# Modulation in quarters, projections behind each quarter, a summed square for two token blocks

## The chip, the cores and the metric

The kernel runs on one core of one Trainium2 chip. The metric is device time in microseconds (us) of one launch, the median of the runs. Before the change it is 1892.64 us (three runs, 1891.05 to 1894.15).

## The reference

One layer of a diffusion backbone runs over 256 context tokens and 2048 latent tokens of 1024 channels. The modulation gives one shift, scale and gate per channel, one set for the latent tokens (from `c`) and one for the context (from `c_ctx`). The input is normalised, scaled and shifted, and projected by one wide matrix; a state-space branch and a convolution branch follow, and an output projection.

```python
silu_ctx, silu_c = silu(c_ctx)[None, :], silu(c)
mod_ctx = silu_ctx @ w_mod[l] + b_mod[l]          # (1, 3*1024); mod_lat the same with silu_c

def trunk_layer(x, mod, grid, h0, ...):
    shift, scale, gate = split(mod, 3)
    h = rms_norm(x, g_pre) * (1 + scale) + shift  # x * rsqrt(mean(x*x) + EPS) * g_pre ...
    u = h @ w_in
    z, xbc, dt_raw, ga, gb, gsil = split(u, ...)
    y_ssd, h_fin = ssd_branch(z, xbc, dt_raw, ...)
    y_conf = conformer_branch(ga, gb, ...) * silu(gsil)
    out = concatenate([y_ssd, y_conf]) @ w_out
    return x + gate * rms_norm(out, g_post), h_fin
```

## The kernel before

Tokens are held in blocks, channels on the 128 partitions. Block 0 is the 256 context tokens; blocks 1 to 4 are 512 latent tokens each. The first half of the program works on blocks 1, 2 and 0, in that order. The 1024 input channels are eight tiles of 128, counted by `k`.

`hprep` (L241) makes the input `h` of one block. Its eight tiles `ht` are loaded (L253), multiplied by the reciprocal root mean square of their tokens (VectorE, L288; the factors stand in a PSUM bank `pr`, which TensorE fills at L278 from the `rstd` columns `xr` that GpSimd makes at L128), scaled and shifted by the modulation `S1` and `SH` (ScalarE, L289), and split into a rounded part `hh` (VectorE, L281) and the rest `hl` (L282, GpSimd, every fourth on VectorE). For block 1 the mean squares come from the tiles themselves: ScalarE squares each (L260), and TensorE sums its partitions with four matmuls against ones (L262, 64 trace records for the block). For all other blocks they come from the same tokens in the other layout: `xin` (L205, 512 KB for each 128 tokens), squared and summed along the row by ScalarE in one instruction (L272).

`modulation(h)` (L207) makes half of the scales and shifts, 512 channels of each. It loads eight 512 KB pieces `wm` of `w_mod`, multiplies them on TensorE into `mp` (L222), copies `mp` out (L228), turns it with eight small transposes into `mc` (L231) and adds the biases on VectorE (L235 to L237).

A projection unit, `xbc_unit` (L434), takes one weight tile and runs 24 matmuls per block (`mm_cm`, L361 to L363: for each `k` the products hh·wh, hl·wh and hh·wl) into a bank `xp`; ScalarE copies that out to `raw` (L446). The weight arrives as two halves `wr` (L335) and is split into `wh` (ScalarE, L336) and `wl` (GpSimd, L337), which are also written to DRAM for later (`whd`, `wld`, L338 and L339). `dt_block` (L299) runs 16 more matmuls per block into `pd` (L306, L307), whose transposes are `pdt` (L316).

At the start (L857 to L888) the order in which the steps are called is written out by hand: the squares of block 1, the first half of the modulation, four tiles of `h`, the second half, and two projection units (`first[0]`, `first[1]`) stepped between. The third unit and `pd` for block 1 come in `xbc_phase` (L466), where the three units go through blocks 2 and 0 while those blocks are prepared. A scheduler turns the calls into one fixed list per engine; each engine works its list strictly in order and waits on semaphores. All loads and stores are issued by SyncE (SP), also in one fixed order, and an issue waits until the eighth transfer before it has landed. `dcol` (L881) is a pair of 2 KB loads made of single 4-byte elements.

Of the kernel before, what the change touches and what calls it, by code (L numbers as in the profile page):

```python
# [67 lines left out]
def backbone_kernel(ctx, tc, xa, xt_in, cols, rows, wconv, conf_b, gp_row, bg_row, state0, w_mod, w_dt, w_in, w_out,  # L68
# [138 lines left out]
    def modulation(h):  # L207

        mp = bank("mm", f"mp{h}")
        for k in range(KT):  # L210
            if h == 1 and k in (4, 5):
                wm = pa.tile([P, 2, 512], F32, tag=("xT", "el")[k - 4], name=f"wm{h}_{k}", bufs=1)
            elif h == 1 and k > 5:
                wm = cp.tile([P, 2, 512], F32, tag="x4", name=f"wm{h}_{k}", bufs=3)
            else:
                w = 2 if h else 4
                if k % w == 0:
                    wms = hps[0 if h else 2].tile([P, w, 2, 512], F32, tag="ab"[k // w], name=f"wm{h}_{k}")
                wm = wms[:, k % w]
            DMA.dma_start(wm, w_mod[k * P:(k + 1) * P, 0:2 * D].rearrange("p (s c) -> p s c", s=2)[:, :, h * 512:(h + 1) * 512])  # L220
            for s in range(4):
                T.matmul(mp[32 * s:32 * s + 2, 0:256], sc[:, :, k], wm[:, s // 2, s % 2 * 256:s % 2 * 256 + 256],  # L222
                         start=(k == 0), stop=(k == KT - 1))
            yield
        mc = bank("ss", f"mc{h}")
        mr = slab(f"mr{h}")
        for s in range(4):
            (V.tensor_copy if s % 2 else S.copy)(mr[0:2, s * 256:(s + 1) * 256], mp[32 * s:32 * s + 2, 0:256])  # L228
            for q in range(2):
                c = 2 * s + q  # L230
                T.transpose(mc[:, 2 * c:2 * c + 2], mr[0:2, c * P:(c + 1) * P], ident[0:2, 0:2])  # L231
        m = mc[:, 0:16].rearrange("p (s k a) -> p s a k", s=2, k=4)
        ks = slice(4 * h, 4 * h + 4)
        bc4 = lambda c: cv[:, c + 4 * h:c + 4 * h + 4].unsqueeze(1).to_broadcast([P, 2, 4])
        V.scalar_tensor_tensor(S1[:, :, ks], m[:, 1], 1.0, bc4(C_BSC), ADD, ADD)  # L235
        V.tensor_tensor(S1[:, :, ks], S1[:, :, ks], bc4(C_GPRE), MUL)
        V.tensor_tensor(SH[:, :, ks], m[:, 0], bc4(C_BSH), ADD)  # L237
        yield


    def hprep(b, out):  # L241
# [13 lines left out]
        if b == 1:  # L255
            pms = [bank("ss", f"pms{t}") for t in range(nt)]
            for k in range(KT):
                load_t(k)
# [1 line left out]
                S.activation(sq, ts[k], AF.Square)  # L260
                for t in range(nt):
                    T.matmul(pms[t][:, 0:1], sq[:, t * P:(t + 1) * P], ones[:, 0:1], start=(k == 0), stop=(k == KT - 1))  # L262
# [2 lines left out]
        for t in range(nt):
            i = o // P + t
            ms = evp.tile([P, 1], F32, tag="ms", name=f"ms{i}", bufs=4)
            if b == 1:
                V.tensor_scalar(ms, pms[t][:, 0:1], 1.0 / D, EPS, MUL, ADD)
            else:  # L270
                xt = xin.pop(i)
                S.activation(xt, xt, AF.Square, accum_out=ms)  # L272
# [6 lines left out]
        def split(k):  # L279
            t = ts.pop(k)  # L280
            V.tensor_copy(hh[:, k, :], t)  # L281
            (V if k % 4 == 3 else G).tensor_tensor(hl[:, k, :], t, hh[:, k, :].bitcast(F32), SUB)  # L282

        for k in range(KT):
            if b != 1:
                load_t(k)
            t = ts[k]
            V.tensor_tensor(t, t, pr[:, :BN], MUL)  # L288
            S.activation(t, t, AF.Identity, bias=SH[:, a, k:k + 1], scale=S1[:, a, k:k + 1])  # L289
            if k > 0 and not (b == 1 and k == 4):  # L290
                split(k - 1)
            if b == 1 and k == 3:
                split(k)
# [571 lines left out]
    for _ in range(4):
        next(prep)
        next(mod)
    next(mod)
    for _ in range(4):
        next(first[0])  # L870
        next(first[1])
        next(mod)
    next(prep)
# [334 lines left out]
```

## Time and profile before

| what | value |
|---|---|
| median of three runs | 1892.64 us (1891.05 to 1894.15) |
| the profiled execution's own time | 1895.74 us |
| its span, first to last instruction | 1894.0 us |
| granted TensorE clock, mean over the span | 0.987 |
| DVE (VectorE), ACT (ScalarE), POOL (GpSimd) busy | 62%, 42%, 33% of the span |
| moved by DMA | 375.30 MB, mean 198 GB/s |

An engine's busy time is the union of its instructions. A timeline row gives start, length, engine, line, tile written and tiles read, and in brackets how long the engine had stood idle and what released it. A time of the span is counted from its first instruction. A matmul's row shows its latency, so the rate is read from one start to the next. The rows that the prediction argues from stand in it.

### The profile page before, as it was taken

The numbers are of one execution on the slowest core, as the hardware profiler recorded it, in microseconds if no ns is written. First come the engines' busy times: TensorE is split into PE (matmuls) and PEld (weight loads), VectorE is DVE, ScalarE is ACT, GpSimd is POOL, SyncE is SP. The second block draws the span as 40 slices with busy tenths as digits, with TensorE's granted clock in tenths as the row PEclk, the third lists the DMA queues.
The fourth block names the chain that finished last, engine by engine and source line by source line (L and its number), as shares of the span: only waits on it lengthen the run. The fifth ranks groups of instructions, "written<-read, shape, count | busy, mean of one in ns | idle before, by whom it ended". The sixth has DMA issues, their size and how long they took to land.

```text
span 1894.0 us, 27057 instructions
## 1 busy us (share of the span) xinstructions
PE 1836.3 (97%) x9739; PEld 1502.5 (79%) x9739; DVE 1174.3 (62%) x1605; ACT 786.4 (42%) x1746; POOL 629.8 (33%) x613
## 2 busy tenths in 40 slices
PE   7999999999999999999999989989999999999998
PEld 5888878888888878888877767767787888888886
DVE  3686873333343443687688778788438677776752
ACT  2546414545444453355245655554314323222321
POOL 2524314445444442301133433342025233333220
PEclk9999999999999999999999999999999999999999
DMA  8656566656566674645777786887777655555532
GB/s 309 224 193 217 200 222 193 200 170 211 191 220 198 219 241 154 190 168 189 195 191 178 235 214 195 248 237 190 240 266 226 200 179 177 159 167 171 171 101 77
DMA packets 290386, 375.30 MB, mean 198 GB/s; under 512 B 85190, under 2 KB 187462, under 8 KB 290252
## 3 DMA queue, kind: packets, MB, share of 16 engines
q1 hardware_dynamic: 290252, 373.58, 63.7%
q8 instruction: 77, 1.26, 0.3%
q14 instruction: 57, 0.47, 0.1%
HBM read 243.92 MB, written 129.59 MB: 197 GB/s over the span
## 4 chain that ended last, share of the span: by engine, by line
PE 66%; DVE 8%; issue 5%; DMA 4%; ACT 2%; POOL 2%; SPq 0%; POOLq 0%; DVEq 0%; ACTq 0%
PE op L1058 19%; PE sp L361 6%; PE sp L362 6%; PE sp L363 6%; DVE cg L573 3%; PE gb L361 2%; PE ga L361 2%; PE ga L362 2%; PE ga L363 2%; PE gb L362 2%; PE gb L363 2%; PE xp L361 2%; PE xp L362 2%; PE xp L363 2%; DMA lb<-lt 2%
## 5 line engine op out<-in xcount | busy, mean ns | idle before, releaser
L361 PE MATMUL sp<-hh,wh 128*128 128x512 f32 (+1 forms) x640 | 239.8, 375 | 0.0
L362 PE MATMUL sp<-hl,wh 128*128 128x512 f32 (+1 forms) x640 | 236.8, 370 | 0.0
L363 PE MATMUL sp<-hh,wl 128*128 128x512 f32 (+1 forms) x640 | 236.5, 370 | 0.0
L668 ACT ACTIVATE lb<-lb,WB 128x128 f32<-128x128 f32 x576 | 181.4, 391 | 97.4 <-POOL lb L660 96.4
L361 PE MATMUL xp<-hh,wh 128*128 128x512 f32 (+1 forms) x480 | 179.1, 375 | 3.8 <-ACT raw L446 2.6
L363 PE MATMUL xp<-hh,wl 128*128 128x512 f32 (+1 forms) x480 | 179.2, 373 | 1.0 <-POOL wl L337 0.6
L362 PE MATMUL xp<-hl,wh 128*128 128x512 f32 (+1 forms) x480 | 179.4, 374 | 0.0
L660 POOL TENSOR_SCALAR_AFFINE_SELECT lb<-lb 128x512 f32<-128x512 f32 x144 | 109.3, 766 | 201.4 <-DMA lb<-lt 127.6
L458 DVE SCALAR_TENSOR_TENSOR cva<-raw,cwh,cva 128x1280 f32<-128x1280 f32 (+1 forms) x96 | 149.2, 1562 | 41.0 <-ACT cva L452 39.3
L337 POOL TENSOR_TENSOR wl<-wr,wh 128x512 fp32r<-128x512 f32 x88 | 129.5, 1484 | 129.6 <-ACT wh L336 119.6
L573 DVE SCALAR_TENSOR_TENSOR cg<-cg,cv 128x256 f32<-128x256 f32 x240 | 138.5, 590 | 3.6
L361 PEld LDWEIGHTS sp<-hh,wh 128*128 128x128 f32 x640 | 121.0, 189 | 22.9 <-issue 3.1
L363 PEld LDWEIGHTS sp<-hh,wl 128*128 128x128 f32 x640 | 120.9, 189 | 20.8
L362 PEld LDWEIGHTS sp<-hl,wh 128*128 128x128 f32 x640 | 121.2, 189 | 19.7
L361 PE MATMUL ga<-hh,wh 128*128 128x512 f32 (+1 forms) x320 | 122.3, 382 | 5.8 <-DMA wh<-whd 5.8
L361 PE MATMUL gb<-hh,wh 128*128 128x512 f32 (+1 forms) x320 | 122.1, 381 | 4.3 <-DVE gth L522 4.3
L533 DVE SCALAR_TENSOR_TENSOR sth<-sth,sp 128x512 f32<-128x512 f32 (+1 forms) x80 | 50.2, 630 | 114.7 <-ACT sth L532 114.6
L362 PE MATMUL ga<-hl,wh 128*128 128x512 f32 (+1 forms) x320 | 120.1, 375 | 0.0
L363 PE MATMUL ga<-hh,wl 128*128 128x512 f32 (+1 forms) x320 | 119.9, 375 | 0.0
L362 PE MATMUL gb<-hl,wh 128*128 128x512 f32 (+1 forms) x320 | 119.8, 374 | 0.0
L363 PE MATMUL gb<-hh,wl 128*128 128x512 f32 (+1 forms) x320 | 119.7, 374 | 0.0
L361 PEld LDWEIGHTS xp<-hh,wh 128*128 128x128 f32 x480 | 91.4, 191 | 20.3 <-ACT raw L446 3.1
(223 smaller groups left out, 4036.7 us busy)
## 6 DMA issues: line engine op xcount, KB each, us to landing
lb<-lt SPq DMA_DIRECT2D x144, 256.0 KB, 4.5
wr<-in_w_in SPq DMA_DIRECT2D x88, 256.0 KB, 4.8
whd<-wh SPq DMA_DIRECT2D x44, 512.0 KB, 3.6
wld<-wl SPq DMA_DIRECT2D x44, 512.0 KB, 4.0
wh<-whd SPq DMA_DIRECT2D x44, 512.0 KB, 5.7
wl<-wld SPq DMA_DIRECT2D x44, 512.0 KB, 5.5
xT<-xb SPq DMA_DIRECT2D x18, 512.0 KB, 5.6
yp<-yg SPq DMA_DIRECT2D x36, 256.0 KB, 4.6
```

The costliest lines, as they stand in the source:

```text
L337: G.tensor_tensor(wl[:, ks, :], wr, wh[:, ks, :].bitcast(F32), SUB)
L361: T.matmul(ps[:, :BN], wh[:, k, :], hh[:, k, :], start=(k == 0), stop=False)
L362: T.matmul(ps[:, :BN], wh[:, k, :], hl[:, k, :], start=False, stop=False)
L363: T.matmul(ps[:, :BN], wl[:, k, :], hh[:, k, :], start=False, stop=(k == KT - 1))
L458: V.scalar_tensor_tensor(a[:, :n], raw[:, t:t + n], cwh[:, ct * 5 + t:ct * 5 + t + 1], a[:, :n], MUL, ADD)
L533: V.scalar_tensor_tensor(th, th, 1.0, ps[:, :BN], ADD, MUL)
L573: V.scalar_tensor_tensor(acc, g[:, t:t + 256], cv[:, w0 + t:w0 + t + 1], acc, MUL, ADD)
L660: G.affine_select(E[g, hq, d], E[g, hq, d], pattern=[[0, 4], [sg, P]], compare_op=ALU.is_ge, fill=NEG, base=0, channel_multiplier=-sg)
L668: S.activation(lb[:, h, :], lb[:, h, :], AF.Exp, bias=WB[:, i, c + h:c + h + 1])
L1058: T.matmul(pso[n], lhs[:, k % 8, :], w[:, n * 512:(n + 1) * 512], start=(k == 0 and m == 0), stop=(k == 15 and m == 2))
```

## The change

The modulation is made in four quarters of 256 channels (two `k` tiles of scale and of shift each). `w_mod` is laid out on the host so that each 512 KB piece is one contiguous 4 KB row per partition, and the gate's third of it becomes an input of its own. The activations `sc` are padded with zeros from 2 to 32 columns, so that each quarter needs one copy `mr` and one 128x128 transpose `mc` where a half had four copies and eight small transposes. For blocks 1 and 2 ScalarE squares the eight tiles, VectorE adds the squares up (seven additions), and four matmuls with ones sum the partitions at the end; block 2 no longer loads its four `xin`. Block 1's multiplication by `pr` is done for all eight tiles ahead of the modulation. Behind each quarter the hand-written order steps the projection units, the third too; no unit is left for `xbc_phase` to step through block 1. `wdr`, `rw` and `dcol` are loaded behind all that.

```diff
-    sc = pa.tile([P, 2, 8], F32, name="sc")
+    sc = pa.tile([P, 32, 8], F32, name="sc")
+    G.memset(sc, 0.0)
...
+    def mod_tiles(q, j):
+        n = f"wm{q}_{j}"
+        if q == 3 and j == 0:
+            return pa.tile([P, 2, 2, 256], F32, tag="xT", name=n, bufs=1)
+        if q == 3 and j == 1:
+            return pa.tile([P, 2, 2, 256], F32, tag="el", name=n, bufs=1)
+        if q == 3:
+            return cp.tile([P, 2, 2, 256], F32, tag="x4", name=n, bufs=3)
...
-    def modulation(h):
+    def modulation(q):
+        mp = bank("ss", f"mp{q}")
+        for j in range(4):
+            wm = mod_tiles(q, j)
+            DMA.dma_start(wm, w_mod[(4 * q + j) * P:(4 * q + j + 1) * P].rearrange("p (k s c) -> p k s c", k=2, s=2))
+            for kk in range(2):
+                k = 2 * j + kk
+                for s in range(4):
+                    T.matmul(mp[32 * s:32 * s + 32, 0:P], sc[:, :, k], wm[:, kk, s // 2, s % 2 * P:s % 2 * P + P],
+                             start=(k == 0), stop=(k == KT - 1))
+        mr = pa.tile([P, P], F32, tag="mr", name=f"mr{q}", bufs=1)
+        V.tensor_copy(mr, mp[:, 0:P])
+        mc = bank("ss", f"mc{q}")
+        T.transpose(mc[:, 0:P], mr, ident)
...
-        if b == 1:
-            pms = [bank("ss", f"pms{t}") for t in range(nt)]
+        if b in (1, 2):
+            sq = ev(f"sq{b}")[:, :BN]
             for k in range(KT):
                 load_t(k)
-                sq = ev(f"sq{k}")[:, :BN]
-                S.activation(sq, ts[k], AF.Square)
-                for t in range(nt):
-                    T.matmul(pms[t][:, 0:1], sq[:, t * P:(t + 1) * P], ones[:, 0:1], start=(k == 0), stop=(k == KT - 1))
+                if k == 0:
+                    S.activation(sq, ts[k], AF.Square)
+                else:
+                    s1 = ev(f"sq{b}_{k}")[:, :BN]
+                    S.activation(s1, ts[k], AF.Square)
+                    V.tensor_tensor(sq, sq, s1, ADD)
+            pms = bank("ss", f"pms{b}")
+            for t in range(nt):
+                T.matmul(pms[:, t:t + 1], sq[:, t * P:(t + 1) * P], ones[:, 0:1], start=True, stop=True)
...
+        if b == 1:
+            for k in range(KT):
+                scale(k)
+            yield
         for k in range(KT):
...
-                    if half == 0 and b == 0 and u is not first[-1]:
+                    if half == 0 and b == 0:
                         continue
...
     next(prep)
-    run(modulation(0))
+    more_w()
+    next(prep)
+    modulation(0)
+    more_w()
+    steps([prep], 2)
+    modulation(1)
+    more_w()
+    steps(first[:2], 2)
+    steps([prep], 2)
+    modulation(2)
+    steps(first[:2], 2)
+    steps(first[2:], 4)
+    steps([prep], 2)
+    modulation(3)
+    steps(first, 2)
+    steps([prep], 2)
+    steps(first, 2)
+    run(prep)
     DMA.dma_start(wdr.rearrange("p k n -> p (k n)"), w_dt)
```

Behind the join named below, the lists of all engines are the same but for a few neighbours that change places. Three pieces of the lists in front of it follow; line numbers in rows of the changed kernel are its own, and a name's first number is the block (in `xin`, `xr` and `ms` the tile of 128 tokens), the second the channel tile; in `xp` and `raw` they are half, unit and block.

ScalarE before, from the first square of block 2's rows (`xin6` is tokens of block 2) to the copies of block 1's first two units:

```order
L272 ACTIVATE xin6_644,ms6_652<-xin6_644 128x1024
L228 COPY mr1_560<-mp1_418 2x256
L336 CAST wh1152_0_474<-wr1152_0_475 128x512
L336 CAST wh1152_0_474<-wr1152_1_479 128x512
L272 ACTIVATE xin7_646,ms7_657<-xin7_646 128x1024
L289 ACTIVATE ht1_4_302<-ht1_4_302,SH_222,S1_221 128x512
L289 ACTIVATE ht1_5_310<-ht1_5_310,SH_222,S1_221 128x512
L289 ACTIVATE ht1_6_318<-ht1_6_318,SH_222,S1_221 128x512
L289 ACTIVATE ht1_7_326<-ht1_7_326,SH_222,S1_221 128x512
```

ScalarE in the changed kernel, the same place, and from there to the last square of block 2:

```order
L287 ACTIVATE xin0_822,ms0_826<-xin0_822 128x1024
L271 ACTIVATE sq2_696<-ht2_0_697 128x512
L274 ACTIVATE sq2_1_702<-ht2_1_700 128x512
L308 ACTIVATE ht1_6_296<-ht1_6_296,SH_222,S1_221 128x512
L308 ACTIVATE ht1_7_301<-ht1_7_301,SH_222,S1_221 128x512
...
L461 COPY raw0_2_574<-xp0_2_1_577 128x512
L274 ACTIVATE sq2_4_717<-ht2_4_715 128x512
L274 ACTIVATE sq2_5_722<-ht2_5_720 128x512
L274 ACTIVATE sq2_6_727<-ht2_6_725 128x512
L274 ACTIVATE sq2_7_732<-ht2_7_730 128x512
```

What moved: a square of block 0's rows (`xin0`) and two of block 2's tiles now stand ahead of the last two tiles of block 1, and four squares of block 2 stand behind the copy that waits for unit 2's last matmul on block 1 (`raw0_2`).

TensorE before, the last factors of block 2 (`pr2`) and what is queued behind them; 22 of the 24 `xp0_2_1` matmuls follow before block 2's first:

```order
L278 MATMUL pr2_680<-ident_209,xr9_670 128x128
L363 MATMUL xp0_2_1_638<-hh1_264,wl1280_0_485 128x512
L361 MATMUL xp0_2_1_638<-hh1_264,wh1280_0_486 128x512
L362 MATMUL xp0_2_1_638<-hl1_265,wh1280_0_486 128x512
...
L316 MATMUL pdt1_765<-ident_209,d4_1_763 128x128 x4
...
L361 MATMUL xp0_0_2_772<-hh2_642,wh1024_0_462 128x512
```

TensorE in the changed kernel, from the last matmul of unit 2 on block 1 to block 2's first (the two `pd1` rows alternate, 16 matmuls in all):

```order
L378 MATMUL xp0_2_1_577<-hh1_265,wl1280_0_454 128x512
L278 MATMUL pms2_735<-ones_218,sq2_696 128x1 x4
L293 MATMUL pr2_750<-ident_209,xr6_742 128x128
L321 MATMUL pd1_787<-hh1_265,wdt_252 128x512
L322 MATMUL pd1_787<-hl1_266,wdt_252 128x512
...
L293 MATMUL pr2_750<-ident_209,xr7_744 128x128
L293 MATMUL pr2_750<-ident_209,xr8_746 128x128
L293 MATMUL pr2_750<-ident_209,xr9_748 128x128
L331 MATMUL pdt1_806<-ident_209,d4_1_804 128x128 x4
...
L376 MATMUL xp0_0_2_813<-hh2_694,wh1024_0_322 128x512
```

What moved: the factors of block 2 stand behind all projections of block 1, three of the four behind `pd1` too, and nothing but four transposes and block 0's two factors stands between them and block 2's first matmul.

SP in the changed kernel, from `dcol` to the last tile of block 2; the two `wg` are pieces of the gate's matrix:

```order
L900 DMA dcol_245<-in_rows 64x8x1 x2
L207 DMA xin0_822<-in_xa 128x1024
L263 DMA ht2_0_697<-in_xt 128x512
L263 DMA ht2_1_700<-in_xt 128x512
L350 DMA wr1280_0_456<-in_w_in 128x512
...
L350 DMA wr1280_1_460<-in_w_in 128x512
L263 DMA ht2_2_705<-in_xt 128x512
L263 DMA ht2_3_710<-in_xt 128x512
L207 DMA xin1_824<-in_xa 128x1024
L556 DMA wg0_2175<-in_w_gate 128x1024
L556 DMA wg1_2603<-in_w_gate 128x1024
L263 DMA ht2_4_715<-in_xt 128x512
```

Before, `dcol` stood behind all of `w_mod` and one weight tile, followed by `xin6`, `whd0`, the first `wr1152`, `wld0` and the second `wr1152`. Those four last ones now stand ahead of `dcol`, between pieces of `w_mod`.

More of the change, by code (lines that the diff above doesn't have):

```diff
@@ L205, in load_x @@
             DMA.dma_start(xin[i], xa[i * P:(i + 1) * P, :])
-    def modulation(h):
[L209 to L238, printed above, removed]
@@ new lines, in mod_tiles @@
+    def mod_tiles(q, j):
[6 more added lines that the diff above has]
+            return cp.tile([P, 2, 2, 256], F32, tag="x4", name=n, bufs=3)
+        if q == 2:
+            if j % 2 == 0:
+                wms[q, j] = hps[0].tile([P, 2, 2, 2, 256], F32, tag="ab"[j // 2], name=n)
+            return wms[q, j - j % 2][:, j % 2]
+        if j == 0:
+            wms[q] = hps[2].tile([P, 4, 2, 2, 256], F32, tag="ab"[q], name=n)
+        return wms[q][:, j]
@@ L253, in load_t @@
             DMA.dma_start(ts[k], xt_in[k * P:(k + 1) * P, o:o + BN])
-        if b == 1:
-            pms = [bank("ss", f"pms{t}") for t in range(nt)]
+        ev_rs = lambda ms, t: rstd_of(evp, ms, f"xr{o // P + t}")
+        if b in (1, 2):
+            sq = ev(f"sq{b}")[:, :BN]
             for k in range(KT):
                 load_t(k)
-                sq = ev(f"sq{k}")[:, :BN]
-                S.activation(sq, ts[k], AF.Square)
-                for t in range(nt):
-                    T.matmul(pms[t][:, 0:1], sq[:, t * P:(t + 1) * P], ones[:, 0:1], start=(k == 0), stop=(k == KT - 1))
+                if k == 0:
[7 more added lines that the diff above has]
+                T.matmul(pms[:, t:t + 1], sq[:, t * P:(t + 1) * P], ones[:, 0:1], start=True, stop=True)
+            m4 = evp.tile([P, 4], F32, tag="ms4", name=f"ms4_{b}", bufs=2)
+            V.tensor_scalar(m4[:, 0:nt], pms[:, 0:nt], 1.0 / D, EPS, MUL, ADD)
+            rs = [ev_rs(m4[:, t:t + 1], t) for t in range(nt)]
         else:
             load_x(b)
[L265 to L271, printed above, removed]
+            for t in range(nt):
+                ms = evp.tile([P, 1], F32, tag="ms", name=f"ms{o // P + t}", bufs=4)
+                xt = xin.pop(o // P + t)
                 S.activation(xt, xt, AF.Square, accum_out=ms)
                 V.tensor_scalar(ms, ms, 1.0 / D, EPS, MUL, ADD)
-            rs.append(rstd_of(evp, ms, f"xr{i}"))
+                rs.append(ev_rs(ms, t))
         yield
@@ L278, in hprep, with scale @@
             T.matmul(pr[:, t * P:(t + 1) * P], rs[t].to_broadcast([P, P]), ident, start=True, stop=True)
-        def split(k):
+        def scale(k):
+            V.tensor_tensor(ts[k], ts[k], pr[:, :BN], MUL)
+        if b == 1:
+            for k in range(KT):
+                scale(k)
+            yield
+        for k in range(KT):
+            if b not in (1, 2):
+                load_t(k)
+            if b != 1:
+                scale(k)
             t = ts.pop(k)
+            S.activation(t, t, AF.Identity, bias=SH[:, a, k:k + 1], scale=S1[:, a, k:k + 1])
             V.tensor_copy(hh[:, k, :], t)
             (V if k % 4 == 3 else G).tensor_tensor(hl[:, k, :], t, hh[:, k, :].bitcast(F32), SUB)
[L284 to L293, printed above, removed]
             yield
-        split(KT - 1)
-        yield
     def dt_block(b, hb):
@@ L540, in gate_rows @@
             wg = big(f"wg{k}")
-            DMA.dma_start(wg, w_mod[k * P:(k + 1) * P, 2 * D:3 * D])
+            DMA.dma_start(wg, w_gate[k * P:(k + 1) * P, :])
             for a in range(2):
@@ L861, in backbone_kernel @@
     first = [xbc_unit(0, ct, hb, tails) for ct in range(NF)]
+    more_w = lambda: wq.append(load_w(*wcols.pop(0)))
+    steps = lambda us, n: [next(u) for _ in range(n) for u in us]
     next(prep)
-    run(modulation(0))
-    DMA.dma_start(wdr.rearrange("p k n -> p (k n)"), w_dt)
[L865 to L873, printed above, removed]
-    for _ in range(4):
-        next(prep, None)
-        next(first[0])
-        next(first[1])
-    run(prep)
+    more_w()
[16 more added lines that the diff above has]
+    run(prep)
+    DMA.dma_start(wdr.rearrange("p k n -> p (k n)"), w_dt)
     DMA.dma_start(rw, rows[0:64].partition_broadcast(P))
```

20 lines of the change are left out of this document (14 added, 6 removed).

## The prediction

> **What bounds the kernel now.** I read the page first, then the windows of the first 90 us, then the timeline of TensorE there, because the lists of the engines differ only up to one point (the join): block 0's first projection matmul.
>
> ```profile
> PE 1836.3 (97%) x9739; PEld 1502.5 (79%) x9739; DVE 1174.3 (62%) x1605; ACT 786.4 (42%) x1746; POOL 629.8 (33%) x613
> PE 66%; DVE 8%; issue 5%; DMA 4%; ACT 2%; POOL 2%; SPq 0%; POOLq 0%; DVEq 0%; ACTq 0%
> ```
>
> ```profile
> 34.83 0.80 PE L361 MATMUL xp<-hh,wh 128*128 128x512 f32 x1 [0.41 <-DVE hh L281]
> ...
> 49.13 0.63 PE L361 MATMUL xp<-hh,wh 128*128 128x512 f32 x1
> 49.55 0.63 PE L362 MATMUL xp<-hl,wh 128*128 128x512 f32 x1
> ...
> 58.01 0.39 PE L361 MATMUL xp<-hh,wh 128*128 128x512 f32 x1
> 58.24 0.39 PE L362 MATMUL xp<-hl,wh 128*128 128x512 f32 x1
> ...
> 65.92 0.71 PE L361 MATMUL xp<-hh,wh 128*128 128x512 f32 x2
> ...
> 86.39 0.28 PE L361 MATMUL xp<-hh,wh 128*128 128x256 f32 x1
> ```
>
> ```profile
> 51.60:86.39 34.79, 34.79 (x159) 28.46 (x158) 26.29 (x45) 20.15 (x35) 22.28 (x21) 1.00 0.65 229
> ```
>
> TensorE is busy 97% of the span and carries 66% of the chain, so a start that brings it to the join earlier or later moves the end by as much. Block 1's first projection matmul starts at 34.83, block 2's at 65.92, and the join is at 86.39. From 51.60 to the join TensorE is never idle (34.79 of 34.79 us). A 512-column matmul takes 0.23 us from start to start there (58.01 to 58.24) and 0.42 us at the half clock (49.13 to 49.55). Whatever the change wins, it must win ahead of 51.60; whatever opens a hole between 51.60 and 86.39 is lost.
>
> **The change part by part.** The first cost is where ScalarE waits for `xin`.
>
> ```profile
> 22.00:32.00 10.00, 7.66 (x92) 3.23 (x84) 5.87 (x12) 1.96 (x4) 1.06 (x1) 1.00 1.05 386
> 32.00:42.00 10.00, 8.40 (x40) 4.10 (x40) 7.20 (x11) 3.41 (x6) 5.62 (x7) 0.66 0.44 150
> ```
>
> ```profile
> 28.21 1.95 SPq L881 DMA_DIRECT2D dcol<-in_rows  x2
> ```
>
> ```profile
> 43.10 1.06 ACT L272 ACTIVATE xin<-xin 128x1024 f32<-128x1024 f32 x1 [6.08 <-DMA xin<-in_xa]
> 44.07 0.18 ACT L272 ACTIVATION_READ_ACCUMULATOR xin<-xin 128x1 f32 x1
> ```
>
> ```profile
> wm<-in_w_mod SPq DMA_DIRECT2D x16, 512.0 KB, 9.8
> ...
> wr<-in_w_in SPq DMA_DIRECT2D x7, 256.0 KB, 8.8
> whd<-wh SPq DMA_DIRECT2D x2, 512.0 KB, 12.6
> wld<-wl SPq DMA_DIRECT2D x2, 512.0 KB, 7.6
> ```
>
> The queue runs full at 386 GB/s until 32 and then at 150 GB/s for 10 us: 3.86 less 1.50 MB is 2.36 MB not moved, a hole of 6.1 us. It follows the issue of the two `dcol` at 28.21, whose 4-byte pieces fill the queue. The `xin` issued right behind them is squared at 43.10, after ScalarE stood idle 6.08 us for it; the row's square and its accumulator read take 1.06 + 0.18 = 1.24 us. After the change `dcol` still stands right ahead of an `xin`, but two `wr` of 256 KB, a `whd` and a `wld` of 512 KB moved ahead of it: 1.57 MB, 4.1 us at 386 GB/s. Were the hole measured from the issue of `dcol`, which the ring of eight lets go some 2 us later than before (an estimate, half of the 4.1), the square would stand at 45.1; pushed by all the bytes, at 47.2. I take 46.
>
> In the changed list block 1's last two tiles stand behind that square and two squares of block 2.
>
> ```profile
> 5.88 1.33 ACT L260 ACTIVATE sq<-ht 128x512 f32<-128x512 f32 x2 [1.24 <-DMA ht<-in_xt]
> ...
> 33.51 2.93 ACT L289 ACTIVATE ht<-ht,SH,S 128x512 f32<-128x512 f32 x4 [1.95 <-DVE S L236]
> ...
> 58.21 1.26 ACT L446 COPY raw<-xp 128x512 f32<-128x512 f32 x2 [2.54 <-PE xp L363]
> ```
>
> ```profile
> 27.64 4.87 DVE L288 TENSOR_TENSOR ht<-ht,pr 128x512 f32<-128x512 f32 x8 [0.83 <-PE pr L278]
> ...
> 39.27 0.68 DVE L282 TENSOR_TENSOR hl<-ht,hh 128x512 fp32r<-128x512 f32 x1
> ...
> 64.14 0.42 DVE L281 CAST hh<-ht 128x512 fp32r<-128x512 f32 x1
> 64.48 0.42 DVE L318 TENSOR_REDUCE DT<-pdt 128x128 f32<-128x256 f32 x1
> ```
>
> ```profile
> 18.71 2.10 POOL L128 TENSOR_TENSOR xr<-ms,nhalf 128x1 f32<-128x1 f32 x4 [16.61 <-DVE ms L269]
> ...
> 36.50 2.81 POOL L282 TENSOR_TENSOR hl<-ht,hh 128x512 fp32r<-128x512 f32 x2 [0.36 <-DVE hh L281]
> ```
>
> ```profile
> 4.78 8.76 PE L262 MATMUL pms<-ones,sq 128*128 128x1 f32 x40 [4.78 <-ACT sq L260]
> ...
> 26.44 1.16 PE L278 MATMUL pr<-ident,xr 128*128 128x128 f32 x8
> ```
>
> Step 1, block 1's end. 46 + 1.24 (the row's square) + 1.33 (two squares) + 0.73 (a quarter of 2.93) + 0.42 (cast) = 49.7 for `hh` of tile 6. Queued behind it on TensorE are 36 projection matmuls: two tiles for units 0 and 1 (12) and all 24 of unit 2. Ten at the half clock after the wait (4.2 us) and 26 at 0.23 (6.0 us) end at 59.9. Unit 2's weights do not hold this up: its second `wr` stands 2.1 MB behind `xin0` (two tiles, `wr`, `whd`, `wld`, `wr`), 5.4 us, and is split before its fifth tile is reached.
>
> Step 2, from there to block 2's first matmul; all of it is one chain. The copy of unit 2 (half of 1.26) 0.6; four squares at 0.67, 2.7; the last addition, between 0.61 (the multiplications, 4.87 / 8) and 0.68 (a subtraction out of SBUF), taken as 0.65; four `pms`, 1.75 (a matmul is two records: 40 records in 8.76 us); the first `xr` 0.53 (2.10 / 4); its `pr` 0.29 (1.16 for four, two records each). That is 66.4. Then 16 `pd`: 3.7 us at the full clock, 6.7 at the half. TensorE has stood idle some 4 us by then, so I take ten slow and six fast, 5.6: 72.0. Three more `pr` 0.9, eight multiplications 4.87, the reduction 0.42 and the cast 0.42: block 2 starts at **78.6 instead of 65.92, 12.7 us later**.
>
> Step 3, block 2 itself. Before, its prepared tiles ran ahead of TensorE. Now the first `hl` comes 1.4 us (2.81 / 2) behind the first `hh`, with four matmuls (0.9 us or more) to fill it, and TensorE restarts at the half clock after another idle stretch of 5 to 6 us. One stretch of slow matmuls as in the row pair at 157.73 below (3.1 us) does half the work in that time and loses 1.5; I add 0.5 for `hl`: **2 us**. Without either it is 0.
>
> ```profile
> 157.73 0.80 PE L361 MATMUL xp<-hh,wh 128*128 128x512 f32 x1 [2.60 <-ACT raw L446]
> 158.32 0.63 PE L362 MATMUL xp<-hl,wh 128*128 128x512 f32 x1
> ...
> 160.81 0.40 PE L362 MATMUL xp<-hl,wh 128*128 128x512 f32 x1
> ```
>
> This row shows the half clock in this kernel: idle 2.60 us, then slow from 157.73 to 160.81. The Trainium skill, page "TensorE: Matmul & The Clock Gate", Part 1 (The HAM clock gate), says that the array's clock is halved after an idle window of about 3.4 us and comes back only after a busy one of that length, and that the windows run freely. By that rule the two idle stretches that the change opens would each cost one slow window at least, some 1.7 us each by its figure (an estimate); a step 2 with 16 fast `pd` and a step 3 of 0 would be the sum without it, 3.4 us less.
>
> The rest I cost at nothing. The 64 `pms` records of block 1 go (8.76 us for the first 40), but TensorE waits for `w_mod` then anyway; block 1's seven additions (4.6 us at 0.65) fall between the landings of the tiles, and if that cover went they would delay only tiles 0 and 1. Earlier quarters let the first projection start up to 5.4 us sooner (four `wm` of 512 KB fewer ahead of it), but block 1's end hangs on step 1, so this is not kept. The four `xin` of block 2 (2.1 MB) go, but two `wg` and an `xin` stand ahead of its last tiles, and these land before the copy of unit 2 at 59.9 lets ScalarE square them. Padding `sc`, one `mr` and one `mc` per quarter, and the new layout are all ahead of `xin0`; their cover is the wait for it.
>
> **Sum.** 12.7 + 2 = 14.7 us later at the join, and the lists behind it are the same. On the profiled execution's 1895.74 us (span 1894.0) that is 1910.4. That execution stands 3.1 us above the median of the runs, 1892.64, so I forecast **1907.3** for the median after.
>
> **The rivals.** *The early start is kept (faster).* If block 1's projections follow the last `w_mod` quarter at once, everything up to the join slides by the 5.4 us of step 1's first projection: 1887.2. It needs block 1's unit 2 to end before about 43.7: the chain of step 2 at full clock is 16.8 us (18.7 less 1.9 for the `pd`), so ending at 49.1 only equals 65.92, and 5.4 us sooner wins it all. Against it: ScalarE's list, which puts `xin0` first, and the hole of 6.1 us, which the trace shows. *The hole is hidden.* If the queue's backlog covers `dcol`, `xin0` is squared near 40, step 1 ends at 54, and with step 2 as worked out the join is 8.7 us late: 1901.3. *No slow clock.* 1.9 us less in step 2, 1.5 in step 3 and 1.9 in step 1 (ten matmuls, 0.19 less each): 9.4 us late, 1902.0. *It is given back.* TensorE stands still later too (2.60 us at 157.73); if such a wait hangs on a transfer that does not slide, it shrinks: 1904.7. *Longer still.* `xin0` at 47.2, all `pd` slow (1.1 more) and a second slow stretch in step 3 (1.5): 3.8 more, 1911.1. That the change does not do what it says is no rival here: the lists show that it does.
>
> **How the numbers follow.** The forecast has 0.50, longer still 0.13, no slow clock 0.13, the hole hidden 0.09, given back 0.08, the early start kept 0.07. A measurement of this kernel can tell about 0.2%, 3.8 us, from no change. The forecast's own range, with the bounds of `xin0` (0.9 below, 1.2 above) and of the slow clock, is 1902 to 1911. I leave out the faster case and half a us of tails, and allow the 1.5 us by which runs scatter about their median: 1898 to 1912. Faster by over 0.2% is the kept start alone, 0.06; within 0.2% is a mixture of it with the hidden hole, 0.07; the rest, 0.87, is slower.
>
> **What would show it.** In the profile after: ScalarE idle several us ahead of the square of `xin0`, at 45 to 47; block 1's last projection near 60; TensorE idle some 4 us ahead of `pms` and 5 to 6 us ahead of block 2's first matmul, near 78.6, with slow matmuls behind each; the join near 101. I am wrong if block 1's projections end before 50, if block 2's tiles are ready when its factors are, or if a wait behind the join shrinks by the shift.

## The result and the profile after

The changed kernel takes 1920.61 us (median of four runs, 1918.43 to 1922.34) beside 1891.85 us for the kernel before in the same comparison: the ratio is 1.0158, with a 95% interval of 1.0139 to 1.0178. It is slower by 28.8 us; the forecast was 14.7 us and 1907.3 us, with a range of 1898 to 1912. The profiled execution took 1921.66 us, its span is 1919.9 us.

The page of the changed kernel, engines and chain:

```profile
PE 1843.9 (96%) x9807; PEld 1497.7 (78%) x9807; DVE 1198.1 (62%) x1619; ACT 786.6 (41%) x1742; POOL 630.8 (33%) x614
PE 67%; DVE 9%; issue 5%; DMA 3%; ACT 2%; POOL 1%; SPq 0%; POOLq 0%; DVEq 0%; ACTq 0%
```

These averages hardly differ from those before. The first 105 us do. ScalarE's timeline there:

```profile
47.40 1.06 ACT L287 ACTIVATE xin<-xin 128x1024 f32<-128x1024 f32 x1 [7.21 <-DMA xin<-in_xa]
...
49.49 1.50 ACT L308 ACTIVATE ht<-ht,SH,S 128x512 f32<-128x512 f32 x2
...
62.26 0.59 ACT L461 COPY raw<-xp 128x512 f32<-128x512 f32 x1 [3.29 <-PE xp L378]
62.74 1.15 ACT L274 ACTIVATE sq<-ht 128x512 f32<-128x512 f32 x2
```

TensorE's, from its wait for block 1's tile 6 to block 2's first projection matmul, and the join (block 0's first matmul):

```profile
50.81 1.65 PE L376 MATMUL xp<-hh,wh 128*128 128x512 f32 x3 [6.31 <-DVE hh L309]
...
66.64 1.39 PE L278 MATMUL pms<-ones,sq 128*128 128x1 f32 x8 [4.41 <-DVE sq L275]
68.90 0.79 PE L293 MATMUL pr<-ident,xr 128*128 128x128 f32 x2 [0.88 <-POOL xr L128]
...
81.70 1.22 PE L376 MATMUL xp<-hh,wh 128*128 128x512 f32 x2 [4.52 <-DVE hh L309]
...
105.04 0.28 PE L376 MATMUL xp<-hh,wh 128*128 128x256 f32 x1
```

VectorE's in between, and the windows from block 1's restart to block 2's first matmul and from there to the join (in a window's row: its length, busy time and instructions of TensorE, its weight loads, VectorE, ScalarE, GpSimd, the granted clock, the DMA's share and GB/s):

```profile
63.41 3.08 DVE L275 TENSOR_TENSOR sq<-sq,sq 128x512 f32<-128x512 f32 x4 [4.25 <-ACT sq L274]
...
76.11 4.87 DVE L296 TENSOR_TENSOR ht<-ht,pr 128x512 f32<-128x512 f32 x8 [7.89 <-PE pr L293]
80.90 0.42 DVE L333 TENSOR_REDUCE DT<-pdt 128x128 f32<-128x256 f32 x1
81.23 8.22 DVE L309 CAST hh<-ht 128x512 fp32r<-128x512 f32 x8
```

```profile
62.30:81.70 19.40, 9.65 (x40) 8.00 (x40) 8.53 (x16) 8.31 (x13) 3.16 (x6) 0.80 0.06 23
81.70:105.20 23.50, 23.50 (x90) 18.70 (x91) 17.67 (x27) 6.78 (x13) 13.06 (x12) 0.87 0.18 51
```

The path of the forecast is there row by row: ScalarE idle 7.21 us ahead of the square of `xin0`, TensorE behind it, then squares, additions, `pms`, `pr`, the eight scales in one stretch of 4.87 us, and TensorE busy half of the 19.40 us. The join is at 105.04 instead of 86.39, 18.7 us later. So some 10 us of the 28.8 are not explained by anything ahead of the join. (The join is read from one trace, the 28.8 us from medians, so this difference is good to a few us.)

Those are in the rate of the matmuls. First and last of the 24 gate projections of block 2 in the first `gb` unit, long behind the join, before and after:

```profile
239.19 0.39 PE L361 MATMUL gb<-hh,wh 128*128 128x512 f32 x1
...
244.40 0.39 PE L363 MATMUL gb<-hh,wl 128*128 128x512 f32 x1
```

```profile
255.76 0.39 PE L376 MATMUL gb<-hh,wh 128*128 128x512 f32 x1
...
261.12 0.40 PE L378 MATMUL gb<-hh,wl 128*128 128x512 f32 x1
```

23 steps take 5.21 us before (0.2265 each) and 5.36 us after (0.2330 each), with the same instructions, no idle time and the full clock. Read over whole groups, the mean of one row of the page, `sp<-hh,wh`, goes from 375 to 379 ns.

### The profile page after: what moved, and what is told of

Its sections match the earlier page's. It is cut to its first block, busy times and chain, and to the rows that moved or that the text cites. A ratio compares the mean times of both kernels' runs of the same rounds, so it can differ in the third digit from the quotient of the medians.

```text
span 1919.9 us, 27203 instructions
## 1 busy us (share of the span) xinstructions
PE 1843.9 (96%) x9807; PEld 1497.7 (78%) x9807; DVE 1198.1 (62%) x1619; ACT 786.6 (41%) x1742; POOL 630.8 (33%) x614
## 3 DMA queue, kind: packets, MB, share of 16 engines
q1 hardware_dynamic: 287628, 371.48, 62.2%
## 4 chain that ended last, share of the span: by engine, by line
PE 67%; DVE 9%; issue 5%; DMA 3%; ACT 2%; POOL 1%; SPq 0%; POOLq 0%; DVEq 0%; ACTq 0%
PE op L1077 19%; PE sp L376 6%; PE sp L377 6%; PE sp L378 6%; DVE cg L588 3%; PE gb L376 3%; PE gb L378 3%; PE gb L377 3%; PE ga L376 2%; PE ga L377 2%; PE ga L378 2%; PE xp L378 2%; PE xp L377 2%; PE xp L376 2%; PE py L719 1%
## 5 line engine op out<-in xcount | busy, mean ns | idle before, releaser
L376 PE MATMUL xp<-hh,wh 128*128 128x512 f32 (+1 forms) x480 | 180.5, 379 | 12.2 <-DVE hh L309 10.8
L473 DVE SCALAR_TENSOR_TENSOR cva<-raw,cwh,cva 128x1280 f32<-128x1280 f32 (+1 forms) x96 | 153.5, 1607 | 42.4 <-ACT cva L467 36.5
L378 PEld LDWEIGHTS sp<-hh,wl 128*128 128x128 f32 x640 | 121.1, 189 | 23.3
L376 PEld LDWEIGHTS xp<-hh,wh 128*128 128x128 f32 x480 | 91.4, 191 | 31.6 <-DVE hh L309 11.7
```

Source lines behind the costliest of these rows:

```text
L376: T.matmul(ps[:, :BN], wh[:, k, :], hh[:, k, :], start=(k == 0), stop=False)
L378: T.matmul(ps[:, :BN], wl[:, k, :], hh[:, k, :], start=False, stop=(k == KT - 1))
L473: V.scalar_tensor_tensor(a[:, :n], raw[:, t:t + n], cwh[:, ct * 5 + t:ct * 5 + t + 1], a[:, :n], MUL, ADD)
```

## The experiments

Two theories stood at first. **Theory:** the loss ahead of the join has two parts, the DMA hole behind `dcol` that holds `xin0`, and the chain that block 2's summed squares put behind block 1's last unit. **Rival 1:** the new start alone costs the time, and block 2's squares nothing. The 10 us behind the join came out of the first four runs, and the later runs are about them.

All totals below are compared with runs of the kernel before in the same session. The join is block 0's first matmul in each trace (before: 86.39). The last column takes 1890 us times (ratio - 1), and from that the shift of the join: what the kernel lost behind the join. The ratio's interval alone makes it uncertain by 2 to 7 us either way.

| kernel | join, us | median, us | ratio to before (95%) | behind the join, us |
|---|---|---|---|---|
| the change | 105.04 | 1920.61 | 1.0158 (1.0139 to 1.0178) | 11.2 |
| a_dc | 98.29 | 1912.12 | 1.0106 (1.0068 to 1.0145) | 8.1 |
| a_rows2 | 92.86 | 1906.26 | 1.0087 (1.0059 to 1.0115) | 10.0 |
| a_rows2_dc | 87.21 | 1900.87 | 1.0061 (1.0040 to 1.0082) | 10.7 |
| b_sq2 | 97.65 | 1901.44 | 1.0057 (1.0040 to 1.0073) | -0.5 |
| b_pad64 | 85.85 | 1897.33 | 1.0031 (1.0019 to 1.0043) | 6.4 |
| a_addr | 102.95 | 1910.77 | 1.0098 (1.0083 to 1.0113) | 2.0 |
| a_rda | 86.79 | 1888.90 | 0.9996 (0.9984 to 1.0009) | -1.2 |
| a_rdae | 84.38 | 1888.40 | 0.9992 (0.9980 to 1.0004) | 0.5 |

The traces alone sort the kernels in the same way. From the join to the end of its own span, b_sq2, a_addr, a_rda and a_rdae take 1799 to 1803 us, and the change, a_dc, a_rows2, a_rows2_dc and b_pad64 take 1809 to 1815. The one trace of before, 1807.6, came from an execution above its median.

**dcol without the hole (a_dc).**

```diff
-    rw = pa.tile([P, 64], F32, name="rw")
+    rw = pa.tile([P, 80], F32, name="rw")
...
-        DMA.dma_start(dcol[j * HD:(j + 1) * HD],
-                      rows[64:80].rearrange("(q j) -> j q", j=2)[j].partition_broadcast(HD))
+        V.tensor_copy(dcol[j * HD:(j + 1) * HD], rw[j * HD:(j + 1) * HD, 64 + j:80:2])
```

> The changed kernel, with dcol copied out of the row tile rw by two VectorE copies instead of loaded in 4-byte pieces; all lists else the same. If the hole in the DMA queue behind dcol is what holds xin0 (theory): xin0's Square starts near 41.4 instead of 47.40, TensorE's 6.31 us idle ahead of hh of tile 6 is gone, part of the half clock behind it too, unit 2 of block 1 ends at 53 to 56 instead of 62.2, and the total is 6 to 10 us below 1920.6: 1911 to 1915. If the bytes ahead of xin0 hold it (rival), the square stays within 1 us of 47.4 and the total within 2 us of 1920.6.

ScalarE and TensorE in this kernel:

```profile
40.56 1.04 ACT L287 ACTIVATE xin<-xin 128x1024 f32<-128x1024 f32 x1
...
54.51 0.58 ACT L461 COPY raw<-xp 128x512 f32<-128x512 f32 x1 [2.96 <-PE xp L378]
```

```profile
74.92 1.22 PE L376 MATMUL xp<-hh,wh 128*128 128x512 f32 x2 [4.52 <-DVE hh L309]
```

The square of `xin0` no longer waits at all, block 1's last copy comes 7.8 us earlier (62.26 to 54.51) and block 2 6.8 us earlier; the total falls by 8.5 us by the medians, 9.8 by the ratios. It was the hole and not the bytes, which are still ahead of `xin0` here. The wait of 4.52 us ahead of block 2 stays: that part is another cause.

**Block 2 from its rows (a_rows2), and both (a_rows2_dc).**

```diff
-        if b in (1, 2):
+        if b == 1:
...
-            if b not in (1, 2):
+            if b != 1:
                 load_t(k)
```

> The changed kernel, with block 2's mean squares from its four xin rows again (as before the change). If the chain behind unit 2 of block 1 (four squares, additions, pms, xr, pr behind pd, eight scales) is the larger part of the loss (theory): pms2 and the idle at 62.2 are gone, but the last pr and the eight scales still stand behind unit 2, so block 2's first matmul comes at 67 to 70 instead of 81.7, the join 12 to 15 us earlier, the total 1905 to 1909. If block 1's late end alone is the loss (rival 1): the total falls by 3 us at most, 1917 to 1921.

> Both edits. Theory: the two losses add up, so both recoveries do: 1897 to 1901, which is still 5 to 9 us above the kernel before, since eight scales in a row stand ahead of block 2's first cast. Rival: the four xin of block 2 (2.1 MB) then come too late and hold the last factor, and the total stays above 1903.

Block 2's first matmul in a_rows2:

```profile
70.02 1.65 PE L376 MATMUL xp<-hh,wh 128*128 128x512 f32 x3 [4.74 <-DVE hh L309]
```

It comes 11.7 us earlier than in the changed kernel, and the join 12.2 us. The idle stretch ahead of `pms` is gone; the one behind the eight scales is not, as expected. Rival 1 allowed 3 us. With both edits the join is at 87.21, 0.8 us behind that of before. Yet this kernel is 0.61% slower, 11 us. The expectation of 5 to 9 us put those on the eight scales, which was wrong: they would have shown in the join.

**The squares alone, on the kernel before (b_sq2).**

```diff
+        elif b == 2:
+            sq = ev("sq2")[:, :BN]
+            for k in range(KT):
+                load_t(k)
+                if k == 0:
+                    S.activation(sq, ts[k], AF.Square)
+                else:
+                    s1 = ev(f"sq2_{k}")[:, :BN]
+                    S.activation(s1, ts[k], AF.Square)
+                    V.tensor_tensor(sq, sq, s1, ADD)
+            p2 = bank("ss", "pms2")
...
-            if b != 1:
+            if b not in (1, 2):
                 load_t(k)
```

> The kernel before, with block 2's summed squares alone. Theory: the summed squares put pms, xr, pr and eight scales behind the last matmul of unit 2 on block 1 whatever the start looks like, so TensorE stands idle 5 to 9 us ahead of block 2 and works at half clock behind that; the join is 9 to 14 us later than 86.39 and the total 1901 to 1906. Rival 1 (only the new start costs time): within 3 us of 1891.9.

TensorE in this kernel:

```profile
74.57 1.22 PE L375 MATMUL xp<-hh,wh 128*128 128x512 f32 x2 [4.61 <-DVE hh L295]
...
97.65 0.28 PE L375 MATMUL xp<-hh,wh 128*128 128x256 f32 x1
```

The join is 11.3 us late and the total 11 us up: the squares make the chain on the old start as on the new one, and rival 1 falls. (The 4.61 us idle ahead of block 2 are a little under the 5 to 9 expected.) And here nothing is lost behind the join. The four kernels with the new start lose 8 to 11 us there, this one none; a 512-column projection matmul takes 0.233 us from start to start in those four, and 0.228 in this one and in the kernel before. What separates the two families is not the work. `ms4` takes 64 bytes in the pool `evp`, and the pools of the `h` tiles and `cp` are stacked below it: in the changed kernel every `hh` and `hl` lies 64 bytes lower. The weight tiles `wh` and `wl` lie above `evp` and did not move.

**The address alone (b_pad64, a_addr).** The first is the kernel before, the second the changed kernel.

```diff
-    evp = ph_h.enter_context(tc.tile_pool(name="evp", bufs=1, side="right"))
+    evp = ph_h.enter_context(tc.tile_pool(name="evp", bufs=1, side="right")); evp.tile([P, 16], F32, name="pad")
```

```diff
-            m4 = evp.tile([P, 4], F32, tag="ms4", name=f"ms4_{b}", bufs=2)
+            m4 = evp.tile([P, 4], F32, tag="ms", name=f"ms4_{b}", bufs=4)
```

> The kernel before, every list the same, with 64 unused bytes per partition more in the pool evp, so that the tiles hh and hl of all blocks (and the pool cp) lie 64 bytes lower in SBUF, as in the changed kernel, whose ms4 takes 64 bytes there. In the four runs of the changed family the total is 10 to 10.5 us further from that of before than the join is, and a 512-column projection matmul takes 0.233 us from start to start against 0.228 in the two kernels on the start of before. Theory (address): this kernel shows 0.233 too, the join within 1 us of before, and a total 8 to 12 us above before, 1898 to 1902. Rival (the work or the order of the new start does it, through the DMA traffic or swapped neighbours): 0.228, and within 3 us of before.

> The changed kernel, with the two ms4 tiles in slots of ms, so that hh and hl lie where they lay before. Theory (address): 0.228 us from start to start, the join within 1.5 us of 105, and 8 to 12 us below 1920.6: 1909 to 1913. Rival: 0.233 and within 3 us of 1920.6.

The same 24 matmuls in b_pad64, and in a_addr:

```profile
236.56 0.39 PE L361 MATMUL gb<-hh,wh 128*128 128x512 f32 x1
...
241.93 0.40 PE L363 MATMUL gb<-hh,wl 128*128 128x512 f32 x1
```

```profile
253.07 0.39 PE L376 MATMUL gb<-hh,wh 128*128 128x512 f32 x1
...
258.29 0.39 PE L378 MATMUL gb<-hh,wl 128*128 128x512 f32 x1
```

5.37 us (0.2335 each) with 64 unused bytes in the kernel before, all lists the same; 5.22 us (0.2270) in the changed kernel without them. The totals follow: b_pad64 is slower by 0.31%, a_addr brings the ratio from 1.0158 to 1.0098, 11 us. Its join, 102.95, is 2.1 us earlier than in the changed kernel, more than the 1.5 that were expected. b_pad64's 1897.33 is just under what was expected (1898 to 1902): shown is that the address costs; its size in this kernel is 6 us, not 10. The rate alone would cost more than either: some 4000 such matmuls behind the join at 5 ns each are 20 us (an estimate from their number in the trace). So a part of it goes into waits that TensorE has anyway; one of them, near 260 us, is shown in the next section.

**All three taken out (a_rda), and the scales spread (a_rdae).** a_rda is a_rows2_dc with `ms4` in slots of `ms`. a_rdae adds:

```diff
-            V.tensor_tensor(ts[k], ts[k], pr[:, :BN], MUL)
+            t = ev(f"hs{k}") if b == 2 else ts[k]
+            V.tensor_tensor(t, ts[k], pr[:, :BN], MUL)
+            ts[k] = t
```

> a_rows2_dc (block 2 from its rows, dcol out of rw), with ms4 in slots of ms. If the loss has three parts (dcol's hole ahead of xin0, the chain of block 2's squares, the address) and no others above 2 us, this one is within 3 us of the kernel before: 1887 to 1893.

> a_rda, with block 2's scaled tiles written to the three slots of ev, so that the fourth multiplication waits for the first tile's hl and the first cast no longer stands behind all eight. Theory: block 2's first matmul comes 2 to 4 us earlier than in a_rda, and with it the join: 1884 to 1889, below before. Rival: eight tiles through three slots are slower than TensorE needs them (2.07 us a tile), and what is won ahead is lost within block 2: same as a_rda.

Three parts are enough: a_rda cannot be told from the kernel before. By the ratios `dcol`, the summed squares and the address are worth 9.8, 13.4 and 11.3 us when each is taken out of the change alone, and 30.6 us together: within the intervals they add up. In a_rdae block 2 starts at 60.86 instead of 63.88 and the join is 2.4 us earlier than in a_rda, but the total is the same within its interval: 2 us are below what these comparisons resolve.

**GpSimd beside VectorE (a_hlV).**

```diff
-            (V if k % 4 == 3 else G).tensor_tensor(hl[:, k, :], t, hh[:, k, :].bitcast(F32), SUB)
+            (V if b == 2 or k % 4 == 3 else G).tensor_tensor(hl[:, k, :], t, hh[:, k, :].bitcast(F32), SUB)
```

> The changed kernel, with all eight hl of block 2 on VectorE instead of six on GpSimd. In the changed kernel the eight casts to hh of block 2 take 8.22 us together, 1.03 each, against 0.42 for a cast by itself. Theory: GpSimd's subtractions, which run at the same time, slow VectorE; without them the casts take 0.42 to 0.5, block 2's last hl is ready 1 to 2 us earlier, the join comes 0 to 2 us earlier and the total stays within 3 us of 1920.6. Rival: the casts are slow for what they read or write, and stay above 0.9.

VectorE in this kernel:

```profile
80.92 2.09 DVE L309 CAST hh<-ht 128x512 fp32r<-128x512 f32 x6
82.93 0.68 DVE L310 TENSOR_TENSOR hl<-ht,hh 128x512 fp32r<-128x512 f32 x1
```

Six casts take 2.09 us, 0.35 each, where GpSimd is silent; in the changed kernel 1.03 each beside GpSimd's subtractions. The contention is shown, and that it costs nothing on this path as well: the join is at 104.78 against 105.04, the 0.3 us by which block 2 started earlier, and the ratio is 1.0162 (1.0138 to 1.0186).

**Which address (b_mixX, b_mixY, b_mixZ, b_mixW, b_all64).** All five are the kernel before with every list the same, and unused bytes between its pools. `wh` and `wl` start 224 bytes above a multiple of 256; so did all `hh` and `hl`. The pads, in bytes: X has 32 in each of `evp`, `hp2` and `hp1`; Y 96 in `evp`, 32 in `hp2`, 64 in `hp0`; Z 128 in `evp` and in `hp2`; W 160 in `evp`, 64 in `hp2`, 32 in `hp0`. b_all64 puts 64 above the weights, so that weights and `h` tiles move together:

```diff
-    wp = ph_h.enter_context(tc.tile_pool(name="wp", bufs=1, side="right"))
+    ph_h.enter_context(tc.tile_pool(name="top", bufs=1, side="right")).tile([P, 16], F32, name="pad"); wp = ph_h.enter_context(tc.tile_pool(name="wp", bufs=1, side="right"))
```

> The kernel before, every list the same, with unused bytes in its pools so that in one run the tiles of different blocks lie differently: blocks 1 and 3 (pool hp1) 64 bytes lower than before, as in the changed kernel (address 32 above a multiple of 128; before 96), blocks 2 and 4 (hp2) 32 bytes lower (64 above), and cp 96 lower. If the address of the moving tile sets the rate: the projection matmuls of blocks 1 and 3 take 0.233 us from start to start, those of blocks 2 and 4 a value of their own, and the two differ within one run, or are both 0.233. If the address of cp (raw, cva) does it, all blocks show one rate. Total 1893 to 1899.

> As b_mixX, with blocks 1 and 3 128 bytes lower than before (96 above a multiple of 128 again), blocks 2 and 4 96 bytes lower (a multiple of 128), cp 192 lower. If the rate goes by the address of the moving tile within 128 bytes: blocks 1 and 3 at 0.228; blocks 2 and 4 at one of the two values. If it goes by cp, or by the address within 256 bytes: blocks 1 and 3 at 0.233. Total 1888 to 1897.

> The kernel before, every list the same, blocks 1 and 3 256 bytes lower, blocks 2 and 4 128 bytes lower. If the address of the moving tile within 256 bytes decides: blocks 1 and 3 at 0.227 (median of gb matmuls from start to start), blocks 2 and 4 at 0.232 to 0.234. If cp or the absolute address decides: all four at 0.232 to 0.234.

> The kernel before, every list the same, blocks 1 and 3 at residue 0 within 256 bytes, blocks 2 and 4 at residue 64. No theory of mine says which is fast; by the residues seen, all four at 0.232 to 0.234.

> The kernel before, every list the same, all pools on the weights' side 64 bytes lower, so that weights and h tiles keep their distance. If the distance between moving tile and weights decides: 0.227, as before. If the moving tile's own address decides: 0.233.

In b_mixZ the first `gb` unit on block 1 (256 bytes lower) and on block 2 (128 lower):

```profile
229.52 0.40 PE L361 MATMUL gb<-hh,wh 128*128 128x512 f32 x1
...
234.76 0.39 PE L363 MATMUL gb<-hh,wl 128*128 128x512 f32 x1
...
240.43 0.40 PE L361 MATMUL gb<-hh,wh 128*128 128x512 f32 x1
...
245.79 0.39 PE L363 MATMUL gb<-hh,wl 128*128 128x512 f32 x1
```

Block 2 in b_all64:

```profile
236.99 0.39 PE L361 MATMUL gb<-hh,wh 128*128 128x512 f32 x1
...
242.21 0.39 PE L363 MATMUL gb<-hh,wl 128*128 128x512 f32 x1
```

Each value is the mean of one block's steps within the `gb` units, 145 to 180 of them, without steps of over 0.25 us:

| distance of `hh`, `hl` from the weights, within 256 bytes | mean of `gb` from start to start, us |
|---|---|
| 0: before, all blocks | 0.2272 to 0.2289 |
| 0: b_mixZ, blocks 1 and 3 | 0.2289 and 0.2296 |
| 0: b_all64, all blocks | 0.2270 to 0.2285 |
| -64: the change, b_pad64, b_mixX blocks 1 and 3 | 0.2330 to 0.2334 |
| -32: b_mixX, blocks 2 and 4 | 0.2329 to 0.2331 |
| -96: b_mixY, blocks 2 and 4 | 0.2339 |
| -128: b_mixY, blocks 1 and 3; b_mixZ, blocks 2 and 4 | 0.2323 to 0.2329 |
| 32 and 96: b_mixW | 0.2331 to 0.2335 |

Two rates stand side by side in one run (b_mixZ: 5.24 us for block 1's 23 steps, 5.36 for block 2's), so it is the tile's own place and not that of `cp`. Within 128 bytes is not it (b_mixY). In b_all64 the `h` tiles lie exactly where the changed kernel has them and run at 5.22 us: it is the **distance from the weight tile**, and 0 within 256 bytes is the only fast one of seven tried. The distance to the tiles of `ev` and `cp` does not decide: in the changed kernel these went down by the same 64 bytes as `hh` and `hl`. `pd` does not show the rule by itself. Its weights `wdt` lie 64 bytes off the `h` tiles before and at distance 0 in the change and in b_pad64, and its matmuls, most of them three or four at a time between projections, take 0.231 us in all three; they take 0.227 and 0.228 in b_all64 and a_rda, where the projections beside them are at 0 too.

The totals: b_mixX 1.0053 (1.0033 to 1.0074), b_mixY 1.0068 (1.0042 to 1.0095), at 1900.34 us above the 1888 to 1897 expected; b_mixZ, b_mixW and b_all64 ran once each and took 1898.0, 1901.6 and 1887.9 us, beside 1890.6 of before.

**The same rule in another place (b_op, a_op).** In the output projection `yh`, `yl`, `ph`, `pl` are the weights and `woh`, `wol` the moving tiles. For `k` 0 to 5 they are at distance 0, for `k` 6 to 15 at -64 or 32, in the kernel before too.

```diff
-    wp = ph_h.enter_context(tc.tile_pool(name="wp", bufs=1, side="right"))
+    ctx.enter_context(tc.tile_pool(name="top", bufs=1, side="right")).tile([P, 8], F32, name="pad"); wp = ph_h.enter_context(tc.tile_pool(name="wp", bufs=1, side="right"))
...
-    wo2 = ph_1.enter_context(tc.tile_pool(name="wo2", bufs=1))
+    wo2 = ph_1.enter_context(tc.tile_pool(name="wo2", bufs=1)); wo2.tile([P, 16], F32, name="pad2")
...
-                p2 = ph_1.enter_context(tc.tile_pool(name="p2", bufs=1))
+                p2 = ph_1.enter_context(tc.tile_pool(name="p2", bufs=1)); p2.tile([P, 48], F32, name="pad3")
```

> The kernel before, every list the same, with unused bytes that put all sixteen tiles of woh and wol and the tiles ph and pl at a multiple of 256 bytes from yh and from each other (before: k 0 to 5 are, k 6 to 15 are not), and that move weights and h tiles of the projections together. If the distance sets the rate: the output projection's 1080 matmuls on k 6 to 15 go from 0.233 to 0.227 us, 6.5 us in all, and the total is 1880 to 1886. If it is something of the projections' pools alone: 0.233 stays, and the total is within 3 us of before.

> a_rdae with the same unused bytes. If the distance sets the rate: 6 to 7 us below a_rdae, 1879 to 1885, faster than the kernel before by 0.3 to 0.5%. If not: as a_rdae, 1885 to 1891.

The groups of `ph` and `pl`, whose `k` are 8 to 15, and of `yh` with `wol`, before and in b_op:

```profile
L1058 PE MATMUL op<-woh,ph 128*128 128x512 f32 x288 | 93.2, 400 | 1.0 <-ACT ph L1049 0.9
L1058 PE MATMUL op<-woh,pl 128*128 128x512 f32 x288 | 91.4, 395 | 0.0
L1058 PE MATMUL op<-wol,yh 128*128 128x512 f32 x288 | 89.4, 391 | 0.0
```

```profile
L1058 PE MATMUL op<-woh,ph 128*128 128x512 f32 x288 | 91.7, 396 | 1.1 <-ACT ph L1049 1.0
L1058 PE MATMUL op<-woh,pl 128*128 128x512 f32 x288 | 89.9, 390 | 0.0
L1058 PE MATMUL op<-wol,yh 128*128 128x512 f32 x288 | 89.0, 390 | 0.0
```

The groups that were all off distance 0 lose 4 to 5 ns a matmul, the one that was mostly on it 1 ns. From start to start the matmuls with `ph` and `pl` go from 0.2331 to 0.2271 us. The windows of that stage, the same instructions at both ends, before and in b_op:

```profile
1481.16:1864.86 383.70, 383.70 (x1862) 318.37 (x1861) 250.41 (x296) 109.36 (x229) 110.58 (x97) 1.00 0.52 160
```

```profile
1475.10:1852.80 377.70, 377.70 (x1861) 318.50 (x1860) 250.44 (x296) 108.97 (x230) 100.13 (x97) 1.00 0.53 162
```

6.0 us less, against 6.5 expected. b_op takes 1883.22 us, ratio 0.9962 (0.9950 to 0.9974); a_op 1882.86 us, ratio 0.9966 (0.9952 to 0.9980). **Both beat both kernels**, b_op with nothing but unused bytes; the other edits of a_op add nothing that can be told.

## Why the prediction was right and wrong

The sign, the place and the mechanism ahead of the join were right; the size was half, and the time is outside the range. Of the 13.3 us between 1907.3 and 1920.61, 4.0 stand at the join and the other 9 behind it.

- **Step 1** (block 1's end at 59.9): `xin0` was squared at 47.40, forecast 46 with an upper bound of 47.2. Pushed by all the bytes was the nearer bound. TensorE then stood idle at 62.2, 2.3 us late. Of these, 1.1 stood at its restart already (50.81 instead of 49.7), and 1.2 came in the 36 matmuls behind it, which took 11.4 us instead of 10.2 at a granted clock of 0.73: a longer stretch at half clock. That the hole is the cause of the wait, a_dc shows.
- **Step 2** (18.7 us from there to block 2's first matmul): measured 81.70 - 62.23 = 19.5. The chain is right in each link. That it belongs to block 2's summed squares, a_rows2 and b_sq2 show.
- **Step 3** (2 us within block 2): 105.04 - 81.70 = 23.3 us instead of 20.5, 2.9 us. The window's granted clock, 0.87 over 23.50 us, is 6.1 us at half clock, which loses 3.0. That is enough; the slow casts that I did not foresee do not add to it (a_hlV). The page "TensorE: Matmul & The Clock Gate" of the Trainium skill, Part 1 (The HAM clock gate), was cited for a slow window behind each idle stretch: the trace agrees, with slow matmuls behind both the 4.41 and the 4.52 us. It does not agree with the length of about 3.4 us: 2.60 us idle in the trace of before and 2.06 us near 274 us in the trace after were followed by 3.4 us at half clock too. The prediction's 3.4 us for the sum without slow windows leave its 0.5 us for `hl` in; with step 3 at 0, as that sentence has it, they are 1.9 + 2.0 = 3.9.
- **The sum at the join**: 14.7 forecast, 18.7 measured. This is a matter of size, 2.3 + 0.8 + 0.9 us; the rival "longer still" had 3.8 us more at the join, and 4.0 came. Its first part came (`xin0` at 47.40) and its third (the longer slow stretch in step 3); its second did not, as some ten of the 16 `pd` were slow, as forecast. That its sum fits is partly luck.
- **The step that failed** is the sentence behind the sum, "the lists behind it are the same", from which the shift was carried on 1:1. The lists are the same, but the matmuls in them are not equally fast: `ms4` moved the `h` tiles by 64 bytes against the weights, and each projection matmul takes 0.233 instead of 0.228 us. What the sum put at nothing behind the join was some 10 us. b_pad64 and a_addr show it from both sides. None of my rivals had a cost without an instruction, a byte moved or a wait.
- **Given back later** (2.60 us at 157.73 in the trace of before): that wait lies between 0.7 and 2.6 us in traces of kernels with the same lists, so it scatters. The wait near 260 us does not. Its rows before, in b_pad64 and in the changed kernel:

```profile
260.23 0.80 PE L361 MATMUL gb<-hh,wh 128*128 128x512 f32 x1 [4.25 <-DVE gth L522]
```

```profile
254.87 0.50 PE L361 MATMUL gb<-hh,wh 128*128 128x512 f32 x1 [1.50 <-DVE gth L522]
```

```profile
274.63 0.50 PE L376 MATMUL gb<-hh,wh 128*128 128x512 f32 x1 [2.06 <-DVE gth L537]
```

It is 4.1 to 4.4 us in all four traces with the old start and distance 0 (before, b_sq2, b_all64, b_op), 0.6 to 2.0 us with the old start and other distances (b_pad64 and the four mixes), and 1.5 to 2.2 us with the new start and distance 0 (a_addr, a_rda, a_rdae, a_op). So some 2 us are given back there, by the slower matmuls and by the new start alike. It is not the shift of the join that is given back, which this rival asked for: a_rda has the join of before and waits 2.15 us.
- Costs taken as nothing ahead of `xin0` (block 1's additions, `sc`, `mr`, the layout) are bounded together: a_rda contains them all and is at 0.9996.

## What to carry to other kernels

A new small tile in a stacked pool moves every tile behind it, and TensorE's rate can follow: compare where weights and moving tiles start, within 256 bytes, before and after any edit of the pools, and read the time from one matmul's start to the next far away from the edit. A statistic that is summed over all tiles before any is scaled turns a pipeline into a chain; it pays only where the engine behind it has other work for the whole chain, and whether it does shows in what is queued between. A load in 4-byte pieces belongs behind every load that something waits for, or out of the queue: here two small copies in its place were worth 8 to 10 us.
